# Layer one's keys, values and gates as block products: seven products of halves for two feature blocks in place of eight

## The chip, the cores and the metric

The kernel runs on one core of one Trainium2 chip. The metric is device time in microseconds for one execution, from the program's start to its end. A profile is one execution taken by the hardware profiler; its span goes from the first to the last instruction. Engines are named as in the profile: PE (TensorE, matmuls), PEld (TensorE's weight loads), DVE (VectorE), ACT (ScalarE), POOL (GpSimd), SP (SyncE, which issues all the DMAs here).

## The reference, cut to what matters

One inference step of a two-layer decoder. 512 prompt tokens and 8 x 4 sample tokens, 544 in all, share the weights; the model's width is 1024. Layer one is a dilated sliding-window attention, layer two an RWKV-7 time mixing; each layer also attends to 256 memory tokens, multiplies the branches by a SiLU gate and projects back.

```python
p = xn @ w_in                          # (544 tokens, 1024) x (1024, 3072) in layer one
qkv = p[..., :A_QKV].reshape(bsz, T, 3, A_HEADS, HEAD_DIM)       # 18 blocks of 128 features: 6 q, 6 k, 6 v
q_mem = p[..., A_QKV:A_QKV + MEM_W]                              # 2 blocks
gate = p[..., A_QKV + MEM_W:]                                    # 4 blocks
...                                    # three groups of four heads, windows 128, 512, 2048, dilations 1, 4, 16
o_mem = cross_attn(q_mem, mem_kv)
h = jnp.concatenate([o, o_mem], axis=-1) * jax.nn.silu(gate)
return h @ w_out, new_rows
```

Everything is float32. The change touches how `xn @ w_in` is computed for the 12 key and value blocks and the 4 gate blocks of layer one.

## The kernel before

**Layout.** Features lie on the partitions, tokens along the free dimension. A feature block is 128 outputs of `w_in`, here called a column: a0 to a5 are queries, a6 to a11 keys, a12 to a17 values, a18 and a19 the memory queries, a20 to a23 the gates. The 544 tokens are two halves of 272 (`HF`), so that one half of a column fits one PSUM bank. The contraction over 1024 inputs is eight tiles of 128 (`kt`).

**A product.** A float32 value is kept as two float32r parts, hi and lo, and a product is hi*hi + lo*hi + hi*lo: three matmuls (`mm1`, lines 313 to 316). The input's parts lie in `xg[h][0]` and `xg[h][1]`, made once per half from x and the norm's weight (lines 475, 476); the token's own scale, `rs[0][h]`, is multiplied in when a column is moved out of PSUM. The weights of a column come as two pieces of 128x512 by DMA; ACT casts a piece to hi (line 306), POOL subtracts to get lo (line 307; `split_piece`). Raw pieces have `RAWB` = 2 buffers, hi and lo `HB` = 3 each.

**A column.** `proj_steps` (line 437) runs 2 token halves x 8 key tiles x 3 = 48 matmuls into two PSUM banks (tag "mm", 2 banks) and calls `evac` for each half. For queries, keys and values that is one DVE instruction, product times `rs` into a tile in which tokens are reordered by dilation (line 516; line 513 for keys and values of the first group, which keep their order). `qkv_column` then sends the tile to DRAM and, for values, transposes it on PE.

**Order.** The code lists the work as: a18, a19; memory keys and values; cross attention, with the query columns; bias tables; the first keys and values of each group (a6, a12, a8, a14, a10, a16); the sample group's scores against cached keys (`sample_keys`); a7, a9, a11; the sample softmax; attention for the first feature block (`attention(0)`); a13, a15, a17; the sample group's turn (transposes of its weights) and values (`sample_values`, line 870); `attention(1)`; the gates a22, a23, a20, a21; then the output projection, in an order written out by hand (`PROGS`). A planner puts the instructions of each engine into a queue by priority (the order in the code) and by a simulated time; on the chip each queue runs in order.

**Caches.** The sample group's cached keys and values come through one set of 128x1024 buffers, tag "cc", `CCB` = 9 of them (line 664). `sample_keys` and `sample_values` need 18 loads each. The values' products for both groups of four samples gather in one PSUM bank (tag "so"). The output weights' tiles (`pwo`, line 916) take the memory that these buffers and the sample scores leave.

**Gates.** Line 930 to 935: product times `rs`, tanh on ACT, two DVE products (the second with the attention's output `o`), a cast on ACT and a subtraction on POOL, which give `h0`, the output projection's input, as hi and lo. After them `share` and `product` (lines 960, 979) do the output projection, first with gates 2 and 3.

Of the kernel before, what the change touches and what calls it, by code (L numbers as in the profile page):

```python
# [29 lines left out]
XRB = 14  # L30
# [18 lines left out]
KB = 6  # L49
CCB = 9  # L50
# [182 lines left out]
def _device(tc, I, O):  # L233
# [59 lines left out]


# [101 lines left out]
    def memory_kv(l, mh, ml, pm, kvpool, ws=None, bank=None):  # L396
        kT[l] = kvpool.tile([128, 2, 256], F32, name=f"mkT{l}")
        vM[l] = kvpool.tile([128, 2, 256], F32, name=f"mvM{l}")
# [26 lines left out]
    SB = pk0.tile([128, 1152], F32, name="SB")  # L425
    SN = pk0.tile([128, 2, 96], F32, name="SN")
    pl = pool(p0, "l0", 1)
    qbd = pl.tile([128, 3, 2, 8, 32], F32, name="qbd")
    kn = pl.tile([128, 3, 2, 32], F32, name="kn")
    vn = pl.tile([32, 3, 256], F32, name="vn")  # L430
    o = pl.tile([128, 4, NT], F32, name="o0")
    pq = pool(pqs, "qkv", 1)
    vt = [pq.tile([128, 4, 256], F32, name=f"vt{g}") for g in range(3)]
# [15 lines left out]

    def proj(wsrc, name, evac, w=None):  # L450
        for _ in proj_steps(wsrc, name, evac, w):
            pass

    nc.sync.dma_start(pv, I["pv"])
    first, second, sums = [], [], []
    with ExitStack() as pro:
        pm = pool(pro, "x", 1)
        raws = [pm.tile([128, 512], F32, name=f"raw{j}") for j in range(4)]
        xs = [[pm.tile([128, 4, HF], F32, name=f"x{h}{i}") for i in range(2)] for h in range(2)]
# [43 lines left out]
    nc.sync.dma_start(sel, I["sel"])  # L503

    qkv = {}

    def qkv_column(kind, g, f):

        t = pq.tile([128, 4, 136], F32, tag="qkv"[kind], bufs=(6, KB, 2)[kind], name=f"t{kind}{g}{f}")

        def evac(h, ps):
            if kind and g == 0:
                nc.vector.tensor_tensor(t.rearrange("p c i -> p (c i)")[:, HALF[h]], ps[:, :HF], rs[0][h], ALU.mult)
                return
            dst = t[:, :, h * 68:h * 68 + 68] if kind else t[:, :, 68 - h * 68:136 - h * 68][:, :, ::-1]
            nc.vector.tensor_tensor(
                dst.rearrange("p c i -> p i c"),
                ps[:, :HF].rearrange("p (i c) -> p i c", c=4),
                rs[0][h].rearrange("p (i c) -> p i c", c=4), ALU.mult)

        mt = kind * 6 + g * 2 + f
        proj(I["w_in_a"][mt], f"a{mt}", evac)
# [130 lines left out]
    with ExitStack() as pb:  # L653
        pm = pool(pb, "mem", 1, side="right")
        hl = pm.tile([128, 2, 8, 256], F32R, name="mhl0")
        for _ in memory_in(0, pm, hl):
            pass
        for _ in memory_kv(0, hl[:, 0], hl[:, 1], pm, pk0):
            pass
    psc = ExitStack()  # L660
    pcache = pool(psc, "cache", 1, side="right")

    def cc(name):
        return pcache.tile([128, 1024], F32, tag="cc", bufs=CCB, name=name)

    with ExitStack() as pb:
# [13 lines left out]
    nc.gpsimd.memset(qbd, 0.0)  # L680
    for f in range(2):
        for g in range(3):
            qkv_column(0, g, f)
# [3 lines left out]
    with ExitStack() as pro:  # L687
        pm = pool(pro, "bias", 1)

        ohp = pm.tile([33, 9 * 256], F32, name="ohp")  # L690
        rel = pm.tile([33, 12], F32, name="rel")
        nc.sync.dma_start(ohp, I["ohp"])
        nc.vector.memset(rel[32:33, :], NEG)
        nc.sync.dma_start(rel[0:32, :], I["rel"])
        bv = pm.tile([4, 9 * 256], F32, name="bv")
        for a, b, g in ((0, 512, 0), (512, 1024, 0), (1024, 1536, 0), (1536, 1792, 0), (1792, 2048, 1), (2048, 2304, 2)):
            ps = ps_t(f"bv{a}")
            nc.tensor.matmul(ps[0:4, :b - a], rel[:, g * 4:g * 4 + 4], ohp[:, a:b], start=True, stop=True)
            nc.vector.tensor_copy(bv[:, a:b], ps[0:4, :b - a])
        bd = pdr.tile([4, 9 * 256], F32, name="bd")  # L700
        nc.sync.dma_start(bd, bv)
# [7 lines left out]
        ohs = pm.tile([128, 1248], F32, name="ohs")  # L709
        bad = pm.tile([32, 1248], F32, name="bad")  # L710
# [4 lines left out]
        for t, n in ((ohs, "ohs"), (bad, "bad"), (negsel, "negsel"), (rel4, "rel4"), (dt4, "dt4")):  # L715
            nc.sync.dma_start(t, I[n])
# [6 lines left out]
        for g, a, b in ((1, 0, 512), (2, 512, 1024), (0, 1024, 1152)):  # L723
            ps = ps_t(f"sb{g}")
            nc.tensor.matmul(ps[:, :b - a], lg[:, g].rearrange("p a b c -> p (a b c)"), ohs[:, a:b], start=True, stop=False)
# [173 lines left out]
    with ExitStack() as pas:  # L899
# [3 lines left out]
        for g in range(3):  # L903
            qkv_column(1, g, 1)
# [1142 lines left out]
```

## Time and profile before

| | |
|---|---|
| median of 3 runs | 800.33 us (792.57 to 802.57) |
| the profiled execution's own time | 796.88 us |
| its span | 794.9 us |
| mean granted TensorE clock | 0.976 |
| PE busy | 740.0 us, 93% |
| DVE, POOL, ACT busy | 444.2, 349.4, 338.3 us |
| DMA | 97.49 MB, mean 123 GB/s |

Times in the profile are from the span's start. In a group's row stand the line, the engine, the operation, the tiles (out<-in), shapes and count, then the time in which at least one of them ran and the mean duration of one, then the engine's idle time before them and what ended it. Matmuls overlap in the array, so a matmul's duration is longer than the distance to the next one; the pace is read from starts. The tiles `hi_a`, `lo_a` and `raw_a` are the weight pieces of layer one's columns; `kc` and `vc` are cached keys and values; `so` is the bank of the sample values.

### The profile page before, as it was taken

To read this page: it belongs to the slowest core of one execution; us is meant where nothing else is said; L and a number is where in the kernel's file an instruction comes from. 1 tells how busy PE (TensorE), PEld (TensorE's weight loads), DVE (VectorE), ACT (ScalarE), POOL (GpSimd) and SP (SyncE) were. 2 spreads that over 40 slices of the span, in tenths; PEclk is the share of its full clock that TensorE was granted. 3 is DMA by queue.
4 is the path that set the end of the run, shared out by engine and by line. 5 is a ranking of instruction groups with operands and counts; after the bars stand their busy time and mean duration, and the time that the engine had idled before them with its cause. 6 is when DMAs were issued, how large, how long until landed. Compare 5 with 4: busy or idle time off the path is not lost.

```text
span 794.9 us, 20301 instructions
## 1 busy us (share of the span) xinstructions
PE 740.0 (93%) x8360; PEld 631.8 (79%) x8360; DVE 444.2 (56%) x1088; ACT 338.3 (43%) x789; POOL 349.4 (44%) x389
## 2 busy tenths in 40 slices
PE   6899999999999969889999999899999999999783
PEld 5877878798976857788888889798888987888663
DVE  7743321218455574652545479837599455785456
ACT  7454421125443464447585348243644423621121
POOL 4642322332220554755444337534455345551447
PEclk9999999999999999999999999999999999999797
DMA  7465359862225571254114421210223222540103
GB/s 251 132 221 180 114 176 310 305 242 84 82 68 218 185 242 42 76 162 134 55 47 149 151 89 61 77 41 16 71 74 108 84 82 82 154 130 19 51 31 114
DMA packets 55697, 97.49 MB, mean 123 GB/s; under 512 B 6607, under 2 KB 21231, under 8 KB 55567
## 3 DMA queue, kind: packets, MB, share of 16 engines
q1 hardware_dynamic: 55604, 96.19, 37.1%
q8 instruction: 66, 1.08, 0.6%
q14 instruction: 27, 0.22, 0.1%
HBM read 82.67 MB, written 13.49 MB: 121 GB/s over the span
## 4 chain that ended last, share of the span: by engine, by line
PE 72%; DVE 12%; POOL 5%; DMA 4%; issue 3%; ACT 3%; SPq 1%; POOLq 0%; DVEq 0%; ACTq 0%
PE b_h L314 2%; PE b_h L315 2%; PE b_h L316 2%; PE o L314 2%; PE Sx L566 2%; PE o L315 2%; PE o L316 2%; PE sc L1400 2%; PE y L1663 1%; PE z L1663 1%; PE o L794 1%; PE ox L590 1%; DMA ug<-ud 1%; PE ptx L582 1%; DMA vc<-in_vc 1%
## 5 line engine op out<-in xcount | busy, mean ns | idle before, releaser
L307 POOL TENSOR_TENSOR lo_b<-raw_b,hi_b 128x512 fp32r<-128x512 f32 x58 | 77.6, 1340 | 119.8 <-ACT hi_b L306 88.2
L307 POOL TENSOR_TENSOR lo_a<-raw_a,hi_a 128x512 fp32r<-128x512 f32 x44 | 56.7, 1290 | 130.2 <-ACT hi_a L306 129.6
L306 ACT CAST hi_a<-raw_a 128x512 fp32r<-128x512 f32 x44 | 27.3, 621 | 61.7 <-DMA raw_a<-in_w_in_a 34.6
L306 ACT CAST hi_b<-raw_b 128x512 fp32r<-128x512 f32 x58 | 36.4, 628 | 38.1 <-PE b_h L316 10.0
L315 PE MATMUL b_h<-xg,lo_b 128*128 128x272 f32 x160 | 46.1, 296 | 2.0 <-POOL lo_b L307 2.0
L314 PE MATMUL b_h<-xg,hi_b 128*128 128x272 f32 x160 | 47.3, 301 | 0.0
L316 PE MATMUL b_h<-xg,hi_b 128*128 128x272 f32 x160 | 46.1, 294 | 0.0
L314 PEld LDWEIGHTS b_h<-xg,hi_b 128*128 128x128 f32 x160 | 29.8, 188 | 3.8 <-issue 2.3
L315 PEld LDWEIGHTS b_h<-xg,lo_b 128*128 128x128 f32 x160 | 29.8, 188 | 3.0 <-POOL lo_b L307 2.4
L1477 DVE TENSOR_TENSOR TX<-T,TT 128x30 f32<-128x30 f32 (+14 forms) x90 | 29.3, 326 | 3.9 <-ACT T L1451 2.2
L1479 DVE TENSOR_TENSOR T<-T,TX 128x30 f32<-128x30 f32 (+14 forms) x90 | 30.0, 333 | 1.8
L316 PEld LDWEIGHTS b_h<-xg,hi_b 128*128 128x128 f32 x160 | 29.8, 188 | 0.5
L1705 POOL TENSOR_TENSOR Sd<-St,DF 128x128 f32<-128x128 f32 x21 | 8.4, 402 | 36.5 <-DVE St L1723 19.0
L1400 PE MATMUL sc<-AR,BK 64*64 64x128 f32 x384 | 18.2, 277 | 1.9 <-DVE bv L1346 1.9
L314 PE MATMUL o<-h,hi_o1a 128*128 128x256 f32 (+1 forms) x64 | 18.7, 293 | 0.9 <-DVE z L1941 0.9
L316 PE MATMUL o<-h,hi_o1a 128*128 128x256 f32 (+1 forms) x64 | 18.4, 290 | 0.9 <-DVE h L1797 0.9
L315 PE MATMUL o<-h,lo_o1a 128*128 128x256 f32 (+1 forms) x64 | 18.4, 288 | 0.0
L786 ACT COPY PT<-pa 128x512 f32<-128x512 f32 x16 | 9.1, 586 | 21.8 <-PE pa L785 17.9
L1663 PE MATMUL y<-UV,SR 64*64 64x64 f32 x384 | 17.3, 242 | 0.0
L1400 PEld LDWEIGHTS sc<-AR,BK 64*64 64x64 f32 x384 | 12.4, 133 | 5.0 <-DVE bv L1346 2.3
L1663 PEld LDWEIGHTS y<-UV,SR 64*64 64x64 f32 x384 | 15.7, 157 | 0.3 <-issue 0.3
L1721 DVE TENSOR_TENSOR St<-z,Sd 128x128 f32<-128x128 f32 x21 | 6.0, 286 | 16.2 <-PE z L1663 11.6
(1066 smaller groups left out, 2796.2 us busy)
## 6 DMA issues: line engine op xcount, KB each, us to landing
raw_b<-in_w_in_b SPq DMA_DIRECT2D x58, 256.0 KB, 2.7
raw_a<-in_w_in_a SPq DMA_DIRECT2D x44, 256.0 KB, 2.8
kc<-in_kc SPq DMA_DIRECT2D x18, 512.0 KB, 6.4
vc<-in_vc SPq DMA_DIRECT2D x18, 512.0 KB, 7.6
out_win<-t SPq DMA_DIRECT2D x12, 272.0 KB, 3.0
x<-in_x SPq DMA_DIRECT2D x8, 272.0 KB, 5.4
xr<-in_x SPq DMA_DIRECT2D x16, 136.0 KB, 4.2
x1d<-z SPq DMA_DIRECT2D x2, 1088.0 KB, 5.2
```

What stands on the lines that cost most here:

```text
L306: nc.scalar.copy(hi, raw)
L307: lo_eng.tensor_tensor(lo, raw, hi.bitcast(F32), ALU.subtract)
L314: nc.tensor.matmul(ps[:, :n], hi, xh, start=first, stop=False)
L315: nc.tensor.matmul(ps[:, :n], lo, xh, start=False, stop=False)
L316: nc.tensor.matmul(ps[:, :n], hi, xl, start=False, stop=last)
L566: nc.tensor.matmul(S[hh][64 * e:64 * e + 64, 0:256], qm[r, f, a:a + 64], kT[l][r, f, :], start=True, stop=True)
L786: nc.scalar.copy(PT[hh], pa.rearrange("p (j q) -> p j q", j=4))
L1400: nc.tensor.matmul(pts[e][unit(c, j, h)[0], a:a + 128], BK[H2[h], j, x, CH[c]], AR[H2[h], j, :, CH[c]], start=True, stop=True)
L1477: nc.vector.tensor_tensor(pd, TP[:, 0:s, s:s + 1].to_broadcast([128, s, w]), TT[:, s:s + 1, s + 1:32].to_broadcast([128, s, w]), ALU.mult)
L1479: nc.vector.tensor_tensor(TP[:, 0:s, s + 1:32], TP[:, 0:s, s + 1:32], pd, ALU.add)
L1663: nc.tensor.matmul(out, lhs, rhs, start=start, stop=stop)
L1705: nc.gpsimd.tensor_tensor(Sd, St, DF[:, :, c:c + 1].to_broadcast([128, 2, 64]), ALU.mult)
```

## The change

Two columns are computed together. Call the weights of column 0 A11 (inputs 0 to 511) and A12 (inputs 512 to 1023), of column 1 A21 and A22; the input's token half h and input half i are B(i,h). The four results are sums of two products each, eight in all. The change uses Winograd's form of Strassen's scheme: seven products, p1 to p7, four sums of weight blocks, sums of input blocks made once, and sums of the products. Each product is a block of 128 features x 512 inputs x 272 tokens, 4 key tiles x 3 = 12 matmuls. The order is p1, p6, p2, p7, p4, p5, p3.

```diff
+    def halves_w(srcs, name):
...
+        a11, a21 = tile("a11", srcs[0][:, 0:512]), tile("a21", srcs[1][:, 0:512])
+        a22, a12 = tile("a22", srcs[1][:, 512:1024]), tile("a12", srcs[0][:, 512:1024])
+        s1 = tile("s1")
+        w = [split_piece(None, f"{name}p1", raw=a11)]
+        nc.gpsimd.tensor_tensor(s1, a21, a22, ALU.add)
+        nc.gpsimd.tensor_tensor(a21, a11, a21, ALU.subtract)
+        nc.vector.tensor_tensor(a11, s1, a11, ALU.subtract)
+        w.append(split_piece(None, f"{name}p6", lo_eng=nc.vector, raw=a11))
+        w.append(split_piece(None, f"{name}p2", raw=a12))
+        nc.vector.tensor_tensor(a12, a12, a11, ALU.subtract)
+        w.append(split_piece(None, f"{name}p7", lo_eng=nc.vector, raw=a21))
+        w.append(split_piece(None, f"{name}p4", raw=a22))
+        w.append(split_piece(None, f"{name}p5", raw=s1))
+        w.append(split_piece(None, f"{name}p3", lo_eng=nc.vector, raw=a12))
+        return w
...
+        def product(k, xh, xl):
+            ps = ps_mm(f"{name}{k}")
+            hi, lo = next(w)
+            for kt in range(4):
+                ws = slice(kt * 128, kt * 128 + 128)
+                mm1(ps, hi[:, ws], lo[:, ws], xh[kt], xl[kt], HF, kt == 0, kt == 3)
+            return ps[:, :HF]
+
+        def plus(a, ps, out=None):
+            if out is None:
+                out = pl.tile([128, HF], F32, tag="u", bufs=UB, name=f"u{name}")
+            nc.vector.tensor_tensor(out, ps, a, ALU.add)
+            return out
...
+        nc.scalar.copy(p1, product("p1", *half(0, 0)))
+        u2 = plus(p1, product("p6", *totals[1]))
+        evacs[0](0, plus(p1, product("p2", *half(0, 1)), p1))
+        u3 = plus(u2, product("p7", *totals[2]))
+        evacs[1](0, plus(u3, product("p4", *half(1, 0))))
+        p5 = product("p5", *totals[0])
+        evacs[1](1, plus(u3, p5, u3))
+        plus(u2, p5, u2)
+        evacs[0](1, plus(u2, product("p3", *half(1, 1)), u2))
```

The sums of the input blocks are made once, on DVE with ACT (`sums_of_halves`, behind the query columns in the code), and split to hi and lo; one of them overwrites `xg[1]`'s first four tiles. The pairs are:

```diff
     for g in range(3):
-        qkv_column(1, g, 0)
-        qkv_column(2, g, 0)
+        qkv_pair((1, g, 0), (2, g, 0))
...
-        for g in range(3):
-            qkv_column(1, g, 1)
+        qkv_pair((1, 0, 1), (1, 1, 1))
+        qkv_pair((1, 2, 1), (2, 0, 1))
...
-        for g in range(3):
-            qkv_column(2, g, 1)
+        qkv_pair((2, 1, 1), (2, 2, 1))
...
-    for j in (2, 3, 0, 1):
...
+    for j in (2, 0):
+        proj2([I["w_in_a"][20 + j + i] for i in range(2)], f"a{20 + j}", gate_evacs[j:j + 2])
```

The six query columns stay as they are. For keys and values of a pair, the step that multiplies by `rs` and reorders the tokens now reads the sum in SBUF and runs on POOL; for queries it stays on DVE. A gate's steps stay on their engines and read SBUF in place of PSUM.

To hold the input blocks and their sums (seven slots, `pt0`), memory is used otherwise:

```diff
-XRB = 14
+XRB = 8
...
-KB = 6
-CCB = 9
+CCB = 6
+R0B = 4
+UB = 3
```

The cache buffers go from 9 to 6. Weight blocks a11, a21 and the sum s1 get four buffers of their own beside the two raw ones; three buffers (`UB`) hold sums of products. The memory keys and values of layer one lie where the attention's bias table comes later, so the table's loads follow the cross attention. The bias of the sample scores is written straight into the score tiles. The one-hot tables from which the biases are made come in pieces of at most 512 columns, each by its own DMA, and the bias goes to DRAM piece by piece too. The tiles of the first keys and queries, and the zeroing of `qbd` on POOL, move ahead of the cross attention. `z`, the output projection's result, and the second half of x for it take the slots when the gates' products are done. A dependency (`hold`) keeps the first input sums and the first weight loads of the pairs from running before the memory's norm.

More of the change, by code (lines that the diff above doesn't have):

```diff
@@ L292, in by_turns, with latest @@
         tc.stamp_issue_order_token(next(i for i in reversed(nc.cur_bb.bb.instructions) if i.engine == ET.PE), token)
+    def latest(engine):
+        return next(i for i in reversed(nc.cur_bb.bb.instructions) if i.engine == engine)
     def split_piece(src, name, hl=None, lo_eng=nc.gpsimd, raw=None):
@@ L448, in proj_steps, with tile @@
                         yield 0.345 * DU, 0
+    def halves_w(srcs, name):
+        def tile(k, src=None):
+            t = (pw.tile([128, 512], F32, tag="raw", bufs=RAWB, name=f"raw_{name}{k}") if k in ("a22", "a12") else
+                 pl.tile([128, 512], F32, tag="r0", bufs=R0B, name=f"r0_{name}{k}"))
+            if src is not None:
+                nc.sync.dma_start(t, src)
+                if k in ("a11", "a21") and not qkv.get((1, 0, 0)):
+                    hold(ET.SP)
+            return t
+        a11, a21 = tile("a11", srcs[0][:, 0:512]), tile("a21", srcs[1][:, 0:512])
[13 more added lines that the diff above has]
+        return w
@@ L458, in _device @@
         raws = [pm.tile([128, 512], F32, name=f"raw{j}") for j in range(4)]
-        xs = [[pm.tile([128, 4, HF], F32, name=f"x{h}{i}") for i in range(2)] for h in range(2)]
+        xs = [[slot(2 * h + i, f"x{h}{i}", 4, F32) for i in range(2)] for h in range(2)]
         for h in range(2):
@@ L519, in evac, with qkv_one, qkv_pair @@
                 rs[0][h].rearrange("p (i c) -> p i c", c=4), ALU.mult)
-        mt = kind * 6 + g * 2 + f
-        proj(I["w_in_a"][mt], f"a{mt}", evac)
+        return t, evac
+    def qkv_one(*column):
+        t, evac = qkv_tile(*column)
+        mt = column[0] * 6 + column[1] * 2 + column[2]
+        proj(I["w_in_a"][mt], f"a{mt}", lambda h, ps: evac(h, ps, nc.vector))
+        qkv_after(*column, t)
+    def qkv_pair(*columns):
+        tiles = [qkv_tile(*column) for column in columns]
+        mts = [kind * 6 + g * 2 + f for kind, g, f in columns]
+        proj2([I["w_in_a"][mt] for mt in mts], f"a{mts[0]}_{mts[1]}", [evac for _, evac in tiles])
+        for column, (t, _) in zip(columns, tiles):
+            qkv_after(*column, t)
@@ L678, in _device @@
             pass
-    nc.gpsimd.memset(qbd, 0.0)
+    pq = pool(pqs, "qkv", 1)
+    vt = [pq.tile([128, 4, 256], F32, name=f"vt{g}") for g in range(3)]
+    pst = pool(pss, "st", 1, side="right")
+    sP = [pst.tile([128, 1248], F32, name=f"sP{bg}") for bg in range(2)]
     for f in range(2):
         for g in range(3):
-            qkv_column(0, g, f)
+            qkv_one(0, g, f)
+    sums_of_halves()
     PB = pb_pool.tile([128, 4, 7 * 64 + 256], F32, tag="PB", bufs=1, name="PB")
@@ L806, in _device @@
     for g in range(3):
-        qkv_column(1, g, 0)
-        qkv_column(2, g, 0)
-    pss = ExitStack()
-    pst = pool(pss, "st", 1, side="right")
-    sP = [pst.tile([128, 1248], F32, name=f"sP{bg}") for bg in range(2)]
+        qkv_pair((1, g, 0), (2, g, 0))
     def sample_keys(bg):
@@ L925, in _device @@
     u = pb_pool.tile([128, 4, NT], F32, tag="PB", bufs=1, name="u0")
-    for j in (2, 3, 0, 1):
+    gate_evacs = []
+    for j in range(4):
         def evac(h, ps, j=j):
```

160 lines of the change are left out of this document (111 added, 49 removed).

## The prediction

> **What bounds the kernel now.** I read the page first (busy shares, slices), then the busy time by stretches of the first layer, then the chain of waits from 225 to 300 us, then the timelines of TensorE, VectorE, GpSimd and SyncE beside it, and last the groups of instructions, for durations. The page:
>
> ```profile
> span 794.9 us, 20301 instructions
> PE 740.0 (93%) x8360; PEld 631.8 (79%) x8360; DVE 444.2 (56%) x1088; ACT 338.3 (43%) x789; POOL 349.4 (44%) x389
> PE   6899999999999969889999999899999999999783
> PEclk9999999999999999999999999999999999999797
> ```
>
> TensorE is busy for 93% of the span, at full granted clock in all but two slices, so taking matmuls away can shorten the kernel. The changed columns lie in slices 6 to 14. By stretches (length, then busy time of PE, PEld, DVE, ACT, POOL, then the granted clock, the DMA share and GB/s):
>
> ```profile
> 80.00:100.00 20.00, 20.00 (x175) 16.17 (x174) 6.94 (x20) 8.76 (x24) 5.99 (x8) 1.00 0.35 111
> ...
> 111.00:187.00 76.00, 76.00 (x642) 63.67 (x641) 18.01 (x36) 16.18 (x32) 23.86 (x26) 1.00 0.72 246
> ...
> 260.00:280.00 20.00, 20.00 (x214) 17.73 (x212) 11.92 (x22) 9.46 (x20) 12.35 (x12) 1.00 0.63 197
> 280.00:300.00 20.00, 13.14 (x87) 9.36 (x87) 12.62 (x24) 11.52 (x28) 10.11 (x9) 0.91 0.63 206
> ```
>
> The stretch 111 to 187 holds nine of the twelve key and value columns (a6 to a12, a14, a16) with the sample keys between them: TensorE never idles, VectorE and GpSimd are busy for 18 and 24 of 76 us. From 260 on GpSimd and VectorE are at about 60%, and after 280 TensorE idles. The chain of waits changes hands there (start, length, what):
>
> ```profile
> 244.16 3.20 PE so L879 x57
> 247.37 7.59 DMA vc<-in_vc
> ...
> 261.34 1.86 PE so L879 x32
> ...
> 263.64 1.43 PE so L888 x24
> ...
> 266.66 0.62 POOL h L935
> ...
> 280.29 1.46 POOL lo_wo L307
> ```
>
> Up to 244 us the chain is TensorE's own queue. Then it waits for the sample group's cached values to be loaded again into buffers just freed, and then runs through GpSimd and VectorE, which split the gates' results and the output weights; the gate columns a23, a20 and a21, on TensorE between 250 and 280, are mostly not on it. So a matmul saved ahead of 244 counts, and one saved behind it does not by itself.
>
> **Matmuls taken away.** Each pair of columns has 84 matmuls (7 products x 4 key tiles x 3) in place of 96. Their pace, from one column on TensorE's timeline:
>
> ```profile
> 125.46 0.39 PE L314 MATMUL a12h<-xg,hi_a 128*128 128x272 f32 x1
> 125.69 0.29 PE L315 MATMUL a12h<-xg,lo_a 128*128 128x272 f32 x1
> ...
> 131.50 0.29 PE L316 MATMUL a12h<-xg,hi_a 128*128 128x272 f32 x1
> 131.71 0.64 PE L824 MATMUL sA<-kc,qbd 128*32 128x512 f32 x4
> ```
>
> The second and the last matmul of the column lie 46 steps apart: 5.81 us / 46 = 0.126 us each. Twelve of them are 1.5 us for a pair. The six pairs of keys and values lie ahead of 244 us: -9.1 us on the path. The two pairs of gates would be -3.0 us of TensorE's time behind it: I count 0.
>
> **Work added to the pairs.** For each pair there are seven splits in place of four and four sums of weight blocks, all 128x512; six sums of products out of PSUM (VectorE) and a copy out of it (ScalarE). The four evictions of a key or value pair go from VectorE to GpSimd, since their source is now in SBUF. Durations:
>
> ```profile
> L307 POOL TENSOR_TENSOR lo_a<-raw_a,hi_a 128x512 fp32r<-128x512 f32 x44 | 56.7, 1290 | 130.2 <-ACT hi_a L306 129.6 <-POOL qbd L528 0.4
> L1013 POOL TENSOR_TENSOR z<-z,xr 128x272 f32<-128x272 f32 x16 | 12.1, 793 | 0.1
> L307 DVE TENSOR_TENSOR lo_a<-raw,hi_a 128x512 fp32r<-128x512 f32 x2 | 1.4, 686 | 3.7 <-ACT hi_a L306 3.7
> L513 DVE TENSOR_TENSOR t<-a6h,rs 128x272 f32<-128x272 f32 x2 | 0.9, 442 | 3.8 <-PE a6h L316 3.8
> L516 DVE TENSOR_TENSOR t<-a8h,rs 128x272 f32<-128x272 f32 x2 | 1.3, 662 | 5.2 <-PE a8h L316 5.2
> ```
>
> GpSimd: four splits and two sums x 1.29 = 7.7 us, against four x 1.29 = 5.2 before. Its evictions have no row, since GpSimd has none of this form; the lower end is the plain 128x272 of 0.79 us, the upper end that times VectorE's ratio for the reordered form, 662/442, so 1.19: four are 3.2 to 4.7 us, and I take 0.9 each, nearer the row of GpSimd itself. GpSimd then has about 11.4 us per pair. VectorE: three splits and two sums x 0.69 = 3.4 us, six sums x 0.44 = 2.7 us. ScalarE, busy for 16 of the 76 us above, takes three casts more.
>
> TensorE's own time for a pair in its stage: the stretch of 76 us and a13, which joins it (6.3 us, as from a12h's first matmul to what follows it), less five pairs x 1.5, is 74.7 us for five pairs, 14.9 each. GpSimd's 11.4 is 77% of that, where it had 31% before. Only three pairs of weight tiles and two PSUM banks stand between the engines, so lateness of one reaches the other: I add 2.5 us over these pairs. The ends are 0 and, from what follows, 6.
>
> VectorE and GpSimd also get in each other's way:
>
> ```profile
> 272.07 1.29 POOL L307 TENSOR_TENSOR lo_a<-raw_a,hi_a 128x512 fp32r<-128x512 f32 x1 [0.25 <-ACT hi_a L306]
> 272.55 1.36 DVE L307 TENSOR_TENSOR wo<-raw_wo,wo 128x512 fp32r<-128x512 f32 x1 [0.28 <-ACT wo L306]
> ```
>
> The VectorE split starts 0.48 us into GpSimd's, and ends at 273.91, 0.55 after GpSimd's end at 273.36: it took twice its 0.69. If every two-input instruction of the one shuts out the other, a pair needs 11.4 + 3.4 = 14.8 us of that shared path (14.3 to 15.9 over the bounds of the eviction), just TensorE's 14.9; five pairs at the upper end lose 5 us, and 1 us more for order gives the 6. [...]
>
> **Cache buffers, nine to six.** The sample values take 18 loads of 512 KB through them. Before:
>
> ```profile
> vc<-in_vc SPq DMA_DIRECT2D x18, 512.0 KB, 7.6
> ...
> 246.04 4.71 SPq L876 DMA_DIRECT2D vc<-in_vc  x8
> ...
> 248.00:252.00 4.00, 4.00 (x48) 3.11 (x45) 1.54 (x5) 0.59 (x1) 0.00 (x0) 1.00 1.01 388
> ...
> 259.02 1.29 POOL L307 TENSOR_TENSOR lo_a<-raw_a,hi_a 128x512 fp32r<-128x512 f32 x1 [23.70 <-ACT hi_a L306]
> ```
>
> Nine are loaded early and nine after 246 us, and the values take from 244.2 to 265.1 (the end of line 888's row in the chain above), 21 us. With six buffers twelve loads come late, in three rounds: a group of 1.9 us frees four, and the next needs 7.6 us to land, so 9.5 a round, 28.5 and the last group of 1.9: 30 us, or +9. By rate alone three more loads are 1.5 MB at the DMA's full rate of that stretch, about +4. Below nothing is excluded only if this chain stays last; if it comes off the path the cost is 0. I take +7, nearer the rounds, because the issue follows the release. The keys' 18 loads go through the same buffers, in a stretch of 76 us with the DMA at 0.72: spread over it they cost nothing, up to +3 if the prefetch of a next group is missed.
>
> **What lies behind the values.** GpSimd stands idle for 23.7 us up to 259 there. TensorE, waiting for values, can do the gate pairs earlier than now, so GpSimd can split the gates' weights and most of their results in that time instead of behind 266: two splits of 1.29 us and some five results, at the 0.79 us of a 128x272, leave the tail, 6.5 us of its GpSimd work. The two gate pairs bring VectorE 2 x 6.1 us more, part of it into the tail. I take -4 (between -7 and +5, the latter if these 6.1 us of the last pair stay behind 266 and fall in line with the output weights' splits).
>
> **The rest, at nothing.** The block sums of the input come in once: 12 of the form below on VectorE and some six splits of 128x544.
>
> ```profile
> L476 DVE SCALAR_TENSOR_TENSOR xg<-x,pv,xg 128x272 fp32r<-128x272 f32 x16 | 10.5, 716 | 0.3 <-ACT xg L475 0.3
> ```
>
> That is 8.6 us and, at twice 0.6 us for each split, some 7 more, ahead of about 118 us. VectorE is busy for 7 of 20 us there (stretch 80 to 100), and the query columns cover it; one total overwrites an input block that the last query column reads, but its product is the fifth of the first pair, 6 us later. Without that cover it costs up to +4. On SyncE the bias tables now come in pieces, some 16 DMAs more; they pass weight loads, which have six raw buffers in place of two. The bias table waits for the cross attention, whose memory keys hold its place, and is read only in the attention behind the key columns. The input's second half is loaded again only after the last gate products; its first reader comes eight output products later. These cost 0.
>
> **Sum.** -9.1 + 2.5 + 7 - 4 = -3.6 us. The profiled execution took 796.9 us, its span and 2.0 around it; the three runs' median is 800.3. So 793.3 for such an execution and 796.7 for the median; I name 796.
>
> **Rivals.**
> *All of TensorE's time comes back.* The values start 9 us earlier, their three rounds find enough else to do, and the pairs never wait. For it: no idle time in 111 to 187, and 21 us of gate matmuls to fill the rounds. Against it: the chain after 244 has no TensorE work that could shrink. -9.1 - 3.0 = -12.1: about 786; with the -4 of the tail as well, 782.
> *The shared path becomes the bound (slower).* VectorE's queue is in order: a sum of products that would free a PSUM bank stands behind a split or weight sum that waits for GpSimd, up to 1.29 us. With its own 0.69 and the sum's 0.44 that is 2.4 us, against 1.5 for a product; in the five products of a pair that have such an instruction, up to 4.5 us lost. It decides from 1.5 us per pair on: there the change gains nothing. Half of it in eight pairs is +18 - 12 = +6, about 804; all of it is +24, 821. [...] For it: the row of 1.36 us; against it: GpSimd is free for a quarter of the time, and the splits may run ahead.
> *Values late, nothing relieved.* +9 with no -4 and 2.5 of stalls: +2.4, 801; I count this with the forecast.
>
> **Chances.** Forecast 0.50; all comes back 0.22; shared path 0.28. The range 785 to 812 takes the forecast with its bounds, most of the first rival and over half of the second. A measurement of this kernel tells about 2% (16 us) from no change: faster 0.06 (784 or less, the first rival with the tail's -4), within 0.82, slower 0.12 (816 or more, the upper part of the second rival).
>
> **What would show it.** The step of the matmuls: 96 fewer of 128x272, and the first `so` group near 236 us instead of 244; if it lies there, stalls were small. [...] Evictions: GpSimd rows of 0.8 to 1.2 us; over 2 us would break the sum. The cache: three waits of TensorE for `vc` or one long chain of them, and 30 us from the first `so` to the last. The tail: GpSimd busy between 236 and 259, and the first output product no later after the last `so` than now. A first pair that waits for the block sums would be a term that I set at 0.

## The result and the profile after

The changed kernel is slightly slower. Its median is 805.4 us beside 797.6 us for the kernel before, a ratio of 1.0093 (1.0066 to 1.0119, 95% interval, 20 runs of each). Beside other runs of the kernel before, on one chip with the experiments, it had 801.6 us and a ratio of 1.0028 (0.9986 to 1.0070). The medians here are over all the executions of a kernel; the ratios leave out those that lay over 1.5% above its quickest. The forecast was 796, 0.5% below the 800.3 us that three executions had given; the range of 785 to 812 holds both results.

The page after: span, matmuls, and the two rows of slices.

```profile
span 800.5 us, 20399 instructions
PE 739.4 (92%) x8264; PEld 627.8 (78%) x8264; DVE 497.0 (62%) x1185; ACT 359.6 (45%) x838; POOL 396.1 (49%) x431
PE   6989998999999968989999999999999999899784
PEclk9999999999999979999999999999999999999686
```

There are 96 matmuls fewer, as the change says, about 12 us at the forecast's 0.126 us each, but TensorE is busy for 739.4 us in place of 740.0. One execution of each does not settle how much came back: a second one of each has 734.0 and 742.5, so that on the mean 4.6 us are gone. Two things to see in the slices: TensorE has an 8 in slice 7, where it had a 9, and the granted clock is lower in slices 15 and 38 to 40.

To find where, I cut both executions at the same points of TensorE's order: first query product, first key product, first `so` product, end of the last `so`, first sum of squares of the output (`ssz`), first product of layer two (`b_h`), end. In a row stand the stretch, its length, then the busy time of PE, PEld, DVE, ACT and POOL, the granted clock, the DMA share and GB/s. Length less PE is TensorE's idle time. Before, by these stretches:

```profile
0.00:46.68 46.68, 36.07 (x258) 32.53 (x259) 32.71 (x62) 27.66 (x58) 25.90 (x26) 1.00 0.58 184
111.33:244.09 132.76, 132.29 (x1412) 111.03 (x1411) 53.76 (x121) 45.25 (x93) 35.93 (x39) 1.00 0.50 170
244.09:265.06 20.97, 20.22 (x290) 14.56 (x291) 7.32 (x20) 5.40 (x12) 1.29 (x1) 1.00 0.70 255
265.06:290.06 25.00, 19.35 (x168) 18.62 (x167) 18.39 (x30) 15.15 (x33) 18.90 (x17) 1.00 0.75 245
290.06:351.40 61.34, 56.26 (x425) 44.87 (x425) 36.02 (x98) 27.25 (x67) 33.62 (x47) 0.97 0.31 101
351.40:794.94 443.54, 411.19 (x5310) 360.90 (x5308) 273.52 (x702) 190.62 (x456) 213.08 (x235) 0.96 0.27 83
```

And after:

```profile
0.00:50.01 50.01, 38.82 (x251) 34.69 (x251) 38.11 (x70) 30.41 (x62) 22.51 (x19) 0.97 0.66 222
114.67:243.32 128.65, 123.18 (x1306) 102.06 (x1305) 87.07 (x176) 56.83 (x120) 78.33 (x78) 1.00 0.54 186
243.32:273.31 29.99, 27.57 (x391) 20.02 (x387) 17.96 (x40) 11.12 (x25) 9.61 (x9) 1.00 0.69 247
273.31:293.11 19.80, 14.15 (x83) 12.83 (x83) 11.40 (x26) 9.56 (x21) 8.24 (x7) 0.78 0.77 250
293.11:355.75 62.64, 56.16 (x425) 45.59 (x425) 38.21 (x101) 30.28 (x74) 36.94 (x50) 0.96 0.35 111
355.75:800.48 444.73, 415.16 (x5310) 363.83 (x5308) 274.11 (x702) 189.37 (x455) 213.26 (x235) 0.95 0.26 83
```

| stretch | forecast | measured (two executions of each kernel) |
|---|---|---|
| start to first query | 0 | 46.7, 48.0 before; 50.0, 49.6 after: +2.5 |
| first key to first `so` | -9.1 + 2.5 = -6.6 | 132.8, 132.8; 128.6, 130.3: -3.3 |
| sample values | +7 | 21.0, 20.5; 30.0, 29.4: +9.0 |
| tail, last `so` to `ssz` | -4 | 25.0, 25.6; 19.8, 18.5: -6.1 |
| `ssz` to layer two | 0 | 61.3, 60.8; 62.6, 63.3: +1.9 |
| layer two | 0 | 443.5, 442.2; 444.7, 443.6: +1.3 |

The query columns between them add 0.4. The sum is +5.7, the difference of the mean spans but for rounding. In the stretch of the pairs TensorE's busy time fell by 9.1 us, from 132.29 to 123.18, the very number of the forecast; its idle time rose from 0.5 to 5.5. That the number fits so well is in part luck, since the two stretches do not hold the same work: 106 matmuls fewer are recorded, where six pairs take away 72. Ten more of the gates' matmuls lie in it, and 49 of the attention's have moved behind it. The experiment with eight products, below, compares like with like.

In the rows that follow a pair is named after its second column: `a_14p` holds the products of a8 and a14, and `hi_a_14p` is the high part of a weight block of theirs, cast on ScalarE. What TensorE waited for in the stretch of the pairs (total, times, longest):

```profile
PE a_14p L319 <- ACT hi_a_14p L311: 1.0, 1, 1.0
PE S L900 <- DVE P L915: 1.0, 1, 1.0
PE sb L873 <- DMA bad<-in_bad: 0.9, 1, 0.9
PE a_17p L319 <- ACT hi_a_17p L311: 0.8, 1, 0.8
PE a_13p L319 <- ACT hi_a_13p L311: 0.6, 1, 0.6
```

The pairs' own waits, with four smaller ones, are 3.5 us; 0.9 is a bias table that now comes in pieces, 1.0 the attention's. The groups of the pairs in the profile after (mean ns behind the bar):

```profile
L648 POOL TENSOR_TENSOR t<-ua,rs 128x272 f32<-128x272 f32 x12 | 11.3, 949 | 5.0 <-DVE ua L501 5.0
L645 POOL TENSOR_TENSOR t<-ua,rs 128x272 f32<-128x272 f32 x6 | 4.7, 781 | 4.9 <-DVE ua L501 4.9
L312 DVE TENSOR_TENSOR lo_a_13p<-r_a_13a,hi_a_13p 128x512 fp32r<-128x512 f32 x2 | 2.4, 1200 | 1.3 <-ACT hi_a_13p L311 1.2
L312 DVE TENSOR_TENSOR lo_a_12p<-r_a_12a,hi_a_12p 128x512 fp32r<-128x512 f32 x2 | 1.4, 684 | 0.1
```

GpSimd's evictions took 0.78 us plain and 0.95 reordered, the 0.9 that I had taken. VectorE's 128x512 split takes 0.68 us in one pair and 1.2 in another, much as the prediction's two rows had it (0.69 and 1.36). On VectorE a12's three splits ran beside no GpSimd instruction and took 0.68, 0.69 and 0.69 us; a13's three each overlapped at least one and took 1.01, 1.40 and 0.90. Not every overlap lengthened a split: a17's first ran beside two short copies and took 0.69. What the longer splits were worth is another matter, and is tested below.

One chain, from the trace after, shows how a pair comes late. Timeline of SyncE, GpSimd, VectorE and TensorE around the pair a15, a17 (start, length):

```profile
189.83 1.29 POOL L312 TENSOR_TENSOR lo_a_13p<-raw_a_13a,hi_a_13p 128x512 fp32r<-128x512 f32 x1 [0.47 <-ACT hi_a_13p L311]
191.15 0.34 SPq L464 DMA_DIRECT2D raw_a_17a<-in_w_in_a  x1
193.89 1.28 POOL L473 TENSOR_TENSOR r_a_17s<-r_a_17a,raw_a_17a 128x512 f32<-128x512 f32 x1 [0.69 <-DMA raw_a_17a<-in_w_in_a]
195.14 0.77 POOL L645 TENSOR_TENSOR t<-ua,rs 128x272 f32<-128x272 f32 x1
195.87 1.30 POOL L312 TENSOR_TENSOR lo_a_17p<-r_a_17a,hi_a_17p 128x512 fp32r<-128x512 f32 x1
197.13 1.28 POOL L474 TENSOR_TENSOR r_a_17a<-r_a_17a,r_a_17a 128x512 f32<-128x512 f32 x1
197.22 0.39 PE L320 MATMUL a_17p<-xg,lo_a_17p 128*128 128x272 f32 x1 [0.23 <-POOL lo_a_17p L312]
...
198.44 1.24 DVE L475 TENSOR_TENSOR r_a_17a<-r_a_17s,r_a_17a 128x512 f32<-128x512 f32 x1 [1.32 <-POOL r_a_17a L474]
```

The load of A22 goes out 0.03 us after a split of the pair before has freed its raw buffer (at 191.12). When it is there, at 193.9, four GpSimd instructions follow in a row, one of them an eviction of the pair before. TensorE waits 0.23 us for the low half that the third makes, and the 0.8 us for a17 above stand behind the fourth, a sum of blocks: VectorE's next sum waits 1.32 us for it, and ScalarE casts the result for TensorE.

The sample values after, from TensorE's timeline; a row is a group of 32 matmuls that reads four buffers and so frees them:

```profile
251.03 1.93 PE L1022 MATMUL so<-vc,sP 128*32 128x256 f32 x32 [1.32 <-DMA vc<-in_vc]
...
261.30 1.93 PE L1022 MATMUL so<-vc,sP 128*32 128x256 f32 x32
...
268.79 1.93 PE L1022 MATMUL so<-vc,sP 128*32 128x256 f32 x32 [0.26 <-DMA vc<-in_vc]
```

The first such group starts at 243.32. The next ones follow after 7.7, 10.3 and 7.5 us, and 4.5 us after the start of the last the values end.

### The profile page after: what moved, and what is told of

The parts are those of the page before. It is cut to its first block, busy times and chain, and to the rows that moved or that the text cites. A ratio compares the mean times of both kernels' runs of the same rounds, so it can differ in the third digit from the quotient of the medians.

```text
span 800.5 us, 20399 instructions
## 1 busy us (share of the span) xinstructions
PE 739.4 (92%) x8264; PEld 627.8 (78%) x8264; DVE 497.0 (62%) x1185; ACT 359.6 (45%) x838; POOL 396.1 (49%) x431
## 4 chain that ended last, share of the span: by engine, by line
PE 58%; DVE 8%; POOL 5%; DMA 4%; issue 3%; ACT 2%; SPq 0%; POOLq 0%; DVEq 0%; ACTq 0%
PE o L319 2%; PE b_h L319 2%; PE o L320 2%; PE o L321 2%; PE b_h L320 2%; PE b_h L321 2%; PE sc L1548 2%; DMA vc<-in_vc 1%; PE y L1811 1%; PE o L943 1%; PE z L1811 1%; POOL lo_b L312 1%; PE Sx L713 1%; PE pa L934 1%; PE ssz L1152 1%
## 5 line engine op out<-in xcount | busy, mean ns | idle before, releaser
L312 POOL TENSOR_TENSOR lo_a<-raw_a,hi_a 128x512 fp32r<-128x512 f32 x12 | 15.6, 1300 | 22.4 <-ACT hi_a L311 15.0
L1869 DVE TENSOR_TENSOR St<-z,Sd 128x128 f32<-128x128 f32 x21 | 6.0, 286 | 18.5 <-PE z L1811 15.8
L312 POOL TENSOR_TENSOR lo_mem<-raw_mem,hi_mem 128x512 fp32r<-128x512 f32 x8 | 11.7, 1469 | 6.7 <-ACT hi_mem L311 6.5
L1457 POOL TENSOR_TENSOR rv<-rv,mhalf 128x10 f32<-128x10 f32 x6 | 13.9, 2324 | 2.0 <-DVE rv L1456 2.0
L1811 PE MATMUL z<-UV,BK 64*64 64x64 f32 x384 | 13.9, 248 | 1.0 <-DVE UV L1851 1.0
```

The costliest lines, as they stand in the source:

```text
L312: lo_eng.tensor_tensor(lo, raw, hi.bitcast(F32), ALU.subtract)
L1457: nc.gpsimd.tensor_tensor(rv[:, 1], rv[:, 0], mhalf.to_broadcast([128, 10]), ALU.pow)
L1811: nc.tensor.matmul(out, lhs, rhs, start=start, stop=stop)
```

## The experiments

The theory was that the cache buffers cost what the seven products save, and that the rest is stalls from GpSimd's load. The rivals were the two raw buffers, VectorE and GpSimd in each other's way, and something outside the changed stages.

| kernel | median us | ratio to the kernel before (95%) | clock over its runs |
|---|---|---|---|
| before, again | 795.9 | 1.0007 (0.9976 to 1.0038) | 0.973 |
| after | 805.4 | 1.0093 (1.0066 to 1.0119) | 0.959 |
| after, again | 801.6 | 1.0028 (0.9986 to 1.0070) | 0.965 |
| before with six cache buffers | 805.4 | 1.0084 (1.0043 to 1.0125) | 0.967 |
| after with eight products | 804.4 | 1.0078 (1.0050 to 1.0106) | 0.969 |
| after, input sums later | 811.1 | 1.0148 (1.0087 to 1.0209) | 0.964 |
| after, nine buffers for the values (V9) | 796.1 | 0.9990 (0.9951 to 1.0030) | 0.970 |
| V9, again | 798.0 | 0.9993 (0.9959 to 1.0027) | 0.969 |
| V9, raw buffers exchanged | 809.9 | 1.0144 (1.0078 to 1.0211) | 0.958 |
| V9, evictions on VectorE | 808.7 | 1.0130 (1.0069 to 1.0191) | 0.961 |
| V9, gates by eight products | 801.9 | 1.0037 (0.9997 to 1.0076) | 0.965 |
| V9, output weights' raw buffers | 808.4 | 1.0151 (1.0102 to 1.0201) | 0.959 |
| after, output weights' raw buffers | 807.7 | 1.0156 (1.0108 to 1.0205) | 0.961 |

**The kernel before with six cache buffers.** One number of the change, alone.

```diff
-CCB = 9
+CCB = 6
```

> The kernel before with six cache buffers in place of nine, nothing else. If the three rounds of loads for the sample values are what costs 9 us there, the time from the first to the last matmul of the sample values goes from 21 to about 30 us; the tail behind them gives some of it back (5 us did come back in the changed kernel), so +3 to +5 us in all. If the gate columns fill the wait and the values are off the path: 0. If the sample keys suffer too, there is idle time of TensorE between 111 and 187 us and more than +5.

Values and tail of this kernel (windows as above):

```profile
247.36:276.88 29.52, 28.68 (x366) 21.80 (x365) 11.12 (x29) 9.09 (x21) 7.57 (x8) 1.00 0.81 286
276.88:298.16 21.28, 14.22 (x91) 13.22 (x90) 12.67 (x21) 10.70 (x23) 10.62 (x9) 0.88 0.65 207
```

The values take 29.5 us, as after; the tail falls to 21.3 us without any gate pair. So +8.8 and -4 both belong to the buffers: TensorE, waiting for values, does the gates earlier (366 matmuls in the stretch of the values in place of 290). By the medians this one number costs as much as the whole change, 0.84%, where +3 to +5 us were expected. The profiled execution, at 799.9 us, is the quickest of its ten.

**The changed kernel with eight products.** All columns singly, no input sums; buffers and memory as after.

```diff
+        for column in columns:
+            qkv_one(*column)
+        return
...
-    sums_of_halves()
...
-        proj2([I["w_in_a"][20 + j + i] for i in range(2)], f"a{20 + j}", gate_evacs[j:j + 2])
+        proj(I["w_in_a"][20 + j], f"a{20 + j}", lambda h, ps, j=j: gate_evacs[j](h, ps[:, :HF]))
```

> The changed kernel's memory and order, but every key, value and gate column by eight products as before, and no sums of input blocks. It keeps six cache buffers, the pieces of the bias tables, the early zeroing, the moved value column. If the layout is what makes the change slow and the seven products still gain something, this is slower than the changed kernel: before +4 (cache), so about 4 us below the changed kernel's excess of 7, that is +3 to +5, if the products as they stand bring a loss of 2 to 4; +8 to +12 if the products bring the 4 us that the stage of pairs shows.

```profile
118.42:251.98 133.56, 133.09 (x1415) 111.36 (x1414) 55.04 (x125) 45.19 (x94) 36.44 (x39) 1.00 0.53 181
251.98:281.81 29.83, 28.82 (x366) 21.75 (x365) 11.11 (x29) 9.10 (x21) 7.58 (x8) 1.00 0.77 272
281.81:302.90 21.09, 14.19 (x89) 13.19 (x89) 12.66 (x21) 10.79 (x23) 10.61 (x9) 0.87 0.58 187
```

It has 804.4 us, no more than after, and lies between the two outcomes that were expected. From the first key to `ssz` it needs 184.5 us, the kernel after 178.4 (128.65 + 29.99 + 19.80). Over this longer stretch both do the same columns, gates and attention, and TensorE's busy time is 176.1 and 164.9 us: 11.2 less, near the 12 of 96 matmuls. Idle time takes 5.2 of them back. The seven products do save 6 us there over the same memory layout. In the whole time these 6 us are not clearly to be found: the kernel after has 805.4 in one set of runs and 801.6 in the other.

**Input sums later.** The sums of halves wait until the memory's keys and values are out of PSUM, on the thought that the sums, on VectorE from 38 us on, push the start back by 3 us.

```diff
-        begun = latest(A).name
         for _ in memory_kv(0, hl[:, 0], hl[:, 1], pm, mkv0):
             pass
+        begun = latest(A).name
```

> The changed kernel with the input's block sums held until the memory's keys and values are out of PSUM (one dependency moved). If the sums on VectorE ahead of the memory values are what delays the first query column by 3.3 us (50.0 in place of 46.7 us), it starts at about 46.7 again and the whole is 2 to 4 us faster than the changed kernel, so +3 to +5 over before. If they then delay the first pair, the gain is lost at 114 us: same as the changed kernel.

The first query product came at 50.3 us, no earlier: the thought was wrong. The pairs' stretch took 140.2 us in place of 128.6; 4.2 of that is work which moved in from the query columns (42 matmuls). The other 7 us are not a wait for the input sums. The idle time is 8.2 us in place of 5.5, and the largest waits in it are 3.2 us for cached keys (`kc`) and 1.4 for a bias sum, while the pairs' own are 3.4, as after; besides, the mean granted clock is 0.98 there in place of 1.00. So the order that came out is worse, but what the input sums cost without their cover, "up to +4" in the prediction, is not shown.

**Nine buffers for the sample values (V9).** The first queries and keys lie, pair by pair, in three buffers that are free by then; three of the values' nine tiles per group use them.

```diff
+    def more(name):
+        t = pqk.tile([128, 2, 4, 136], F32, tag="qk", bufs=3, name=name)
+        return t.rearrange("p a c i -> p (a c i)")[:, 0:1024]
...
-            vc = [cc(f"vc{bg}{j}{b4}").rearrange("p (r c) -> p r c", r=4) for b4 in range(4)]
+            vc = [(more if j and b4 > 1 else cc)(f"vc{bg}{j}{b4}").rearrange("p (r c) -> p r c", r=4) for b4 in range(4)]
...
-        vc0 = cc(f"vc0{bg}").rearrange("p (b c) -> p b c", b=4)
+        vc0 = more(f"vc0{bg}").rearrange("p (b c) -> p b c", b=4)
```

> The changed kernel with three more buffers for the sample values, in the memory of the first queries and keys, which attention has done with by then: nine in all. If the third round of loads costs 9 us, the values take about 21 us in place of 30, and the last one ends near 264 in place of 273; the tail behind then takes back what it had given (5 us), so 3 to 5 us faster than the changed kernel in all. If the values are limited by the rate of the DMA, they take 26 us or more.

```profile
114.38:244.99 130.61, 124.74 (x1307) 103.62 (x1305) 86.91 (x176) 57.38 (x120) 77.84 (x78) 0.99 0.57 196
244.99:264.73 19.74, 18.84 (x302) 11.95 (x300) 11.33 (x28) 5.41 (x12) 1.30 (x1) 1.00 0.67 254
264.73:300.87 36.14, 23.36 (x172) 20.93 (x171) 26.74 (x41) 18.30 (x39) 25.07 (x20) 0.86 0.65 213
361.63:794.81 433.18, 406.17 (x5310) 357.30 (x5308) 274.16 (x702) 188.97 (x455) 215.19 (x235) 0.97 0.27 85
```

The values take 20 us again, and the time equals that of the kernel before. The way there is not the expected one. The tail grew to 36.1 us, so from the first key to `ssz` V9 needs 186.5 us, 8 more than after and than before (178.7). What makes it good is the last row: layer two takes 433 us, 10 to 12 less than in either kernel, with the same 5310 matmuls.

**V9 with the raw buffers exchanged.** A11 and A12, free after the second and last split, go into the two buffers that the single columns share; A21, A22 and the sum into the four others.

```diff
-            t = (pw.tile([128, 512], F32, tag="raw", bufs=RAWB, name=f"raw_{name}{k}") if k in ("a22", "a12") else
+            t = (pw.tile([128, 512], F32, tag="raw", bufs=RAWB, name=f"raw_{name}{k}") if k in ("a11", "a12") else
```

> The version with nine cache buffers for the sample values, with the roles of the raw weight buffers exchanged: the two buffers that are shared with the single columns now hold A11 and A12, which are free again after the second and the last split, and the four others hold A21, A22 and the sum. Chain theory (the pairs' 5.9 us of idle TensorE come from a pair's loads waiting for the last splits of the pair before): idle time between the first key product and the first sample value falls to 2 to 3 us, that stretch from 130.6 to 127 to 128, time 793 +- 2. Shared-path theory (VectorE and GpSimd shut each other out): idle stays at 5 to 6, time 796 +- 1.5.

Waits of TensorE from the first key to the first `so` in this kernel:

```profile
PE sA L971 <- DMA kc<-in_kc: 2.7, 2, 1.6
PE a_17p L319 <- ACT hi_a_17p L311: 0.8, 1, 0.8
...
```

The pairs' own waits fall from about 3.6 us in V9 to 1.4 (0.8 and two of 0.3); those at a14, a13 and a9 are gone. So the raw buffers are the larger part of them, the chain theory. But the cached keys, whose loads were hidden before, are now late by 2.7 us, so that idle time falls only from 5.9 to 4.1; and the time is 809.9, not 793: the start, the tail and layer two take 3, 3 and 9 us more than in V9.

**V9 with the evictions on VectorE.**

```diff
-        def evac(h, src, eng=nc.gpsimd):
+        def evac(h, src, eng=nc.vector):
```

> The version with nine cache buffers for the sample values, with the keys' and values' evictions back on VectorE: 24 instructions of 0.8 to 0.95 us leave GpSimd, 24 of about 0.45 to 0.7 come to VectorE. Shared-path or GpSimd theory: idle TensorE between the first key product and the first sample value falls from 5.9 us to 2 to 3, VectorE's splits come back towards 0.7 us, time 793 +- 2. Chain theory: idle stays within 1.5 us of 5.9, time 796 +- 1.5. A third way: VectorE, which also empties PSUM, becomes late: idle over 8, time 799 or more.

Its groups of VectorE's splits, and its waits of TensorE in the same stretch:

```profile
L312 DVE TENSOR_TENSOR lo_a_13p<-r_a_13a,hi_a_13p 128x512 fp32r<-128x512 f32 x2 | 1.4, 708 | 0.0
```

```profile
PE pa L938 <- DVE P L926: 2.0, 3, 1.0
PE a_13p L319 <- ACT hi_a_13p L311: 1.8, 1, 1.8
```

With the evictions off GpSimd most of VectorE's splits are back at 0.7 us, from 1.0 to 1.2; the pair of a9 stays at 1.0, and one split of a17's takes 1.7. Idle time stays at 6.3 us, as the chain theory has it, though the time is 808.7 and not 796; layer two alone takes 448.1 us here. The pairs' own waits go down by about 1 us, and the attention now waits 2 us for VectorE. With GpSimd's evictions VectorE's splits do take longer (a13's two of the form above 1.21 us each on the mean in V9, 0.71 here), but these splits were not what TensorE waited for.

**V9 with the gates by eight products.** The gate columns come singly, in the order of the kernel before. Four input tiles that the gates of the second half read hold a sum of blocks here, so this kernel computes other gates with the same instructions.

```diff
-    for j in (2, 0):
-        proj2([I["w_in_a"][20 + j + i] for i in range(2)], f"a{20 + j}", gate_evacs[j:j + 2])
+    for j in (2, 3, 0, 1):
+        proj(I["w_in_a"][20 + j], f"a{20 + j}", lambda h, ps, j=j: gate_evacs[j](h, ps[:, :HF]))
```

> The version with nine cache buffers for the sample values, with the four gate columns by eight products each, one after the other as in the kernel before; keys and values stay in pairs. That version has 36.1 us from the last sample value to the first sum of squares of the output, the kernel before 25.0. Theory G (the gate pairs bring their results late, in one lump behind the values): the stretch falls to 27 to 31 us although TensorE has 3 us more to do, time 792 +- 2. Theory W (the output weights' loads and splits set it): 33 to 37, time 796 to 799.

The tail falls from 36.1 to 29.5 us with more matmuls in it: the gate pairs do make it late. The time is 4 to 6 us longer all the same, since layer two takes 440.8 us in place of 433.2.

**The output weights' raw buffers.** In V9 the first output weight that is needed is loaded only at 275.9 us, because it shares its raw buffer with the gate pairs. Here it uses the other output weights' three; once on V9, once on the kernel after.

```diff
-            wo.append(weights(src, f"wo{mt}", eng) if mt > 2 else split_piece(src, f"wo{mt}", None, eng))
+            wo.append(weights(src, f"wo{mt}", eng) if mt >= 0 else split_piece(src, f"wo{mt}", None, eng))
```

> The version with nine cache buffers for the sample values; the raw pieces of the first three output weights now use the three buffers of the other output weights in place of the two that they share with the gate pairs. In that version the first piece needed is loaded only at 275.9 us, behind four later pieces, because its buffer waits for the gate pair's last splits. Theory W (this sets the tail): the first piece is loaded near 268, the stretch from the last sample value to the first sum of squares falls from 36.1 to 28 to 31 us, TensorE's idle time in it from 12.8 to 6 to 8; time 788 to 792. Theory O (VectorE's and GpSimd's queue in the tail sets it, the weights only follow): 34 to 37, time 795 to 797.

> The changed kernel with that one edit to the output weights' raw pieces and nothing else. Its tail has 5.6 us of idle TensorE, 3.0 of them at the second output weight. Theory W: idle time in the tail falls by 2 to 3 us, time 800 to 803. Theory O: no difference beyond 1 us, 802 to 805.

On V9 the loads start at 269.8 and the tail falls to 30.7 us, idle time in it from 12.8 to 8.7, about as the first theory has it. But layer two takes 447.6 us, 14 more than in V9, and the kernel is 12 us slower. On the kernel after, the tail becomes 4 us longer and the time 807.7: no gain there.

**Both kernels and V9 again.** Three repeats, for what changes from execution to execution.

> The changed kernel as it is, a second time, for the granted clock and for the scatter of the stages. So far its runs had a mean granted clock of 0.959 and the kernel before 0.972, and within each kernel a hundredth of clock goes with about 5 us. Theory A (the lower clock belongs to this kernel): 0.957 to 0.961 again, beside 0.97 for the kernel before; time 803 to 807. Theory B (the lower clock was chance or the chip): 0.965 to 0.972 and then about 800. Stages of layer one as in the first profile within 1 us: pairs 128.6 us from the first key product to the first sample value, values 30.0.

> The kernel before as it is, a second time. In the profiles so far every edited kernel, also the one with nothing but six cache buffers, has its first query product 3 to 6 us later than the kernel before (46.7 us), and 18 us of TensorE's time at a lower granted clock come and go behind it. Theory S (the start scatters from execution to execution): here it lies anywhere between 46 and 51 us. Theory P (every edit makes the order at the start worse): 46.7 +- 0.5. The stages behind it as in the first profile within 1 us: 132.8 us from the first key product to the first sample value, values 21.0, tail 25.0. Mean granted clock over the runs 0.970 to 0.974.

> The version with nine cache buffers for the sample values as it is, a second time. It was the only edited kernel that was not slower than the kernel before, and in its profile the part from layer two's first product to the end took 433 us, against 439 to 448 in the others, with the same instructions. Theory K (each kernel's own order of layer two fixes its idle time and its clock): 431 to 436 us again, mean granted clock over the runs 0.968 to 0.972, ratio 0.995 to 1.003. Theory E (execution to execution scatter): 438 to 446 us, and a ratio between 1.000 and 1.008. In both the sample values take 20 us and the stretch behind them 36.

The stages of one kernel agree within 2 us. The start lies at 46.7 and 48.0 us before, at 50.0 and 49.6 after: part scatter (the second execution of before has a clock of 0.93 there), part not. V9's layer two takes 431.4 us, on another chip than its first time. So 431 to 433 us belong to V9, as 442 to 445 do to the two others. The list of layer two's matmuls is the same in all of them. Their order is not: the planner puts each engine's queue together anew for each program. By their starts in the traces, 312 of some 5300 stand at another place after than before, 1555 in V9; the two executions of a kernel agree, but for one exchange of neighbours in V9.

All those 312 lie in the first part of layer two. From 627.4 us on before, and 629.0 after, all five engines have the same instructions in the same order. This second part, for before, its repeat, after and its repeat:

```profile
627.40:794.94 167.54, 142.37 (x2208) 124.89 (x2207) 102.21 (x262) 46.55 (x104) 79.29 (x89) 0.93 0.27 83
628.71:794.52 165.81, 139.83 (x2208) 122.92 (x2207) 102.14 (x262) 46.51 (x104) 79.32 (x89) 0.95 0.27 84
629.03:800.48 171.45, 146.50 (x2211) 127.97 (x2211) 103.44 (x262) 46.59 (x104) 79.06 (x89) 0.90 0.26 82
627.89:800.23 172.34, 145.25 (x2211) 128.21 (x2211) 103.33 (x262) 46.59 (x104) 79.13 (x89) 0.90 0.26 81
```

It is 5.2 us longer after, 4.8 of them busy time of TensorE at a lower granted clock. The first part, where the order differs, is 4.0 us shorter after (276.0 and 276.4, against 273.3 and 271.2). So the new order gained in layer two, and the clock took more than that. Over all the kernels here layer two takes from 431 to 448 us, and even the one number of the first experiment gave 439.

**Time at equal clock.** Within each kernel, time falls by 5.2 us for each 0.01 of mean granted clock (191 runs, each kernel's own mean taken off). Brought to 0.970 by this, the means are 799.2 before, 799.4 after (30 runs), 804.1 with six buffers alone, 803.6 with eight products, 797.4 for V9 (22 runs). At equal clock, by this line, the buffers cost 5 us, the seven products give 4 back, and the change is worth nothing; the rest of its loss goes with its lower clock, 0.961 over its 30 runs against 0.973 (77 runs): 6 us. That is a correlation; no experiment sets the clock. And it does not cover single executions: the two repeats had a clock of 0.970 before and 0.969 after and still lay 5.6 us apart (796.5 and 802.0 us), where one execution is off that line by some 2 us.

## Why the prediction was wrong, by its own steps

**Matmuls taken away**: right. TensorE's busy time in the stage fell by 9.1 us, with some luck, since its work is not quite the same; over the same layout and the same work, through the tail, it fell by 11.2 for all eight pairs, where -9.1 and -3.0 were forecast, and that stretch is 6 us shorter.

**Work added to the pairs**: too small. Idle time rose by 5.0 us (6.2 in the repeat) in place of 2.5; the upper end was 6. The durations were right (evictions 0.78 and 0.95 us, splits up to 1.2 on the mean of a pair's row), and GpSimd's added work, 42 us in the stretch for six pairs and the blocks of the first gate pair, is near the 6.2 us per pair forecast. The reason given was not the main one: it named three pairs of weight tiles, two banks and the shared path. In V9 the exchange of raw buffers took away over half of the pairs' own 3.6 us, the move of the evictions about 1. The bias table in pieces, set at nothing, costs 0.9.

**Cache buffers, nine to six**: the mechanism was right, three rounds and 30 us from the first `so` to the last (30.0 and 29.4). The term was +7 and measured +9.0, or +8.8 with this edit alone; the upper end was the rounds' own count, and that was the answer. That it came out so exactly is luck: the rounds took 7.7, 10.3 and 7.5 us in place of 9.5 each, and 4.5 us follow the start of the last group in place of 1.9.

**What lies behind the values**: right in sign, -6.1 for -4. Some 4 us come with the six buffers alone; the gate pairs have no need to be there. When the values are early, as in V9, they make the tail longer.

**The rest, at nothing**: this is the step that failed. It holds +6.1 us: start +2.5, query columns 0.4, the output's end +1.9, layer two +1.3. I had priced what the edits do, and neither that every queue is planned anew behind them nor that TensorE's clock can come out lower. In layer two the two go against each other: the part with a new order is 4.0 us shorter, and the part whose instructions and order are unchanged 5.2 us longer, at a clock of 0.90 in place of 0.93 and 0.95. Between `ssz` and layer two a wait of 2.6 us for ScalarE's `sqoz` came up, which was 0.2 before; at the start the idle time is 11.2 and 12.0 us against 10.6 and 9.4. Why the clock is lower stays open, and so does what of the other stages' part is order and what is clock, and why the start is later with six buffers alone too (49.7 us).

**Sum.** -9.1 + 2.5 + 7 - 4 gave -3.6 in the stages; they measured -3.3 + 9.0 - 6.1 = -0.4. With +6.1 outside, the change is slower: of the miss of 9.3 us, 3.2 lie in the terms of the sum and 6.1 in what stood at nothing. The forecast's 796 also starts from 800.3 us, the median of three executions, while the rivals are counted from about 798; over 20 executions the kernel before has 797.6, from where the same -3.6 gives 794.

**Rivals.** "All of TensorE's time comes back" fell with the pairs' idle time. "Shared path becomes bound" asked for 1.5 us lost per pair; the pairs' waits are 0.6 us each on the mean. Its total, 804, is near the result, but not for its reason. "Values late, nothing relieved" gave 801; the values were as late as it says, but the tail was relieved. That 801 lies near the repeat's 801.6 is luck too.

## What to carry to other kernels

Price what a change takes away to make room for itself with the same care as its arithmetic: here three buffers fewer cost about as much as 96 matmuls fewer give. Where a planner orders the queues, run an edit that changes nothing but one size beside the real one; if that alone moves the untouched part by several microseconds, gains below that can't be argued from the changed stage. And read the granted clock beside busy time, in more than one execution: the same matmuls in the same order, in the second part of layer two, kept TensorE busy for 141 us before and 146 after.

## What the runs showed of the hardware that was not expected

In the trace of each of the two kernels TensorE's granted clock is 0.50 in some stretches and 1.00 between them. Before, six of the stretches last 3.41 us, one 6.83, and one goes from 784.77 us to the end; after, three last 3.41, three 6.83, two 10.24, and one goes from 789.65 to the end. Windows of the kernel before, around the tail's end, with the granted clock in the third last column:

```profile
284.70:288.00 3.30, 0.25 (x3) 0.03 (x1) 2.26 (x5) 2.31 (x6) 1.98 (x2) 1.00 0.61 191
289.80:293.20 3.40, 3.40 (x18) 1.83 (x19) 0.91 (x2) 1.57 (x4) 3.40 (x3) 0.51 0.69 236
293.20:296.60 3.40, 3.40 (x30) 2.53 (x24) 2.65 (x7) 2.49 (x6) 0.10 (x1) 0.99 0.57 157
```

And of the kernel after:

```profile
284.40:287.80 3.40, 3.03 (x12) 2.73 (x13) 1.64 (x3) 2.66 (x6) 2.23 (x2) 0.51 0.96 347
287.80:291.20 3.40, 1.78 (x8) 1.46 (x7) 0.91 (x2) 0.58 (x2) 2.27 (x3) 0.50 1.01 321
291.20:294.60 3.40, 3.15 (x14) 2.04 (x15) 2.27 (x5) 3.25 (x9) 1.03 (x1) 0.50 0.70 252
```

Before, 3.3 us with 0.25 of work end 1.8 us ahead of one such stretch; TensorE is busy through it and through the window behind it, with 18 matmuls in the one and 30 in the other, though not all of one size. Matmuls of 128x272 start 0.22 us apart in it (at 291.74, 291.96 and 292.19 us) and 0.125 apart ahead of it. After, three windows in a row are at half clock, with TensorE busy for 3.03, 1.78 and 3.15 of their 3.40 us. What brings the clock down and what brings it back is not shown by these rows.

Much of the time at half clock lies in the second part of layer two, 23.8 of 37.5 us before and 34.7 of 62.0 after; the mean clock of that part stands in the four rows above: 0.93 and 0.95 before, 0.90 and 0.90 after. The instructions and their order are the same there, so the order of that part is not the reason. Why the clock falls more often after is open: it was seen, not produced by an edit.
